# Gathers tied to chunk products by a one-column copy, and the prompt's odd projections spread over rounds

## The chip, the cores and the metric

The kernel runs on one core of one Trainium2 chip, as a single program of some 71,600 instructions. The metric is the device time of one execution in microseconds: the median over several executions. The five engines are named as the profile names them: PE is TensorE (PEld its weight loads), DVE is VectorE, ACT is ScalarE, POOL is GpSimd, SP is SyncE. Each works through its own instructions in order; between engines, semaphores hold an instruction back until what it reads is written.

## What is computed

The reference is one step of a trunk with two layers over two token groups: 128 prompt tokens (P) and 512 sample tokens (S), 1024 features each, in fp32. Every layer has a mixer and then an expert mixer ("PEER"). Layer 0's mixer is a Fourier and short convolution mixer; layer 1's ("odd") is a recurrence (RG-LRU) and a bidirectional RWKV-7 scan. The part that matters is the expert mixer: 16,384 experts, each one row of a table `u` and one of a table `v`; every token picks 8 x 16 of them.

```python
def _peer(h, wq, keys, u_tab, v_tab):
    ...
    idx = e1 * N_KEYS + e2                 # 8 x 16 experts per token
    gate = jax.nn.softmax(sc, axis=-1)
    def block(args):                       # 128 tokens at a time
        hb, ib, gb = args
        act = jax.nn.gelu(jnp.einsum('td,thkd->thk', hb, u_tab[ib]))
        return jnp.einsum('thk,thkd->td', gb * act, v_tab[ib])

def _rwkv_mix(z, mu, ...):                 # odd layer; z is a projection of the normed tokens
    zp = jnp.pad(z, ((0, 0), (1, 1), (0, 0)))
    z = z + mu * (0.5 * (zp[:, 0:S] + zp[:, 2:S + 2]) - z)
    r, k, v = z[..., 0:o1], z[..., o1:o2], z[..., o2:o3]
    wd, ad, gd = z[..., o3:o4], z[..., o4:o5], z[..., o5:]
```

## The kernel before

**Two ways through the experts.** Sample blocks 1 to 3 (384 tokens) go through all 16,384 experts densely. The prompt's block and sample block 0 (128 tokens each) gather: for each of 128 slots, one indirect DMA brings one row of `u` or `v` per token (128 x 1024 fp32, 0.52 MB) into a tile `g`, and VectorE reduces it: a dot product with the token's input for `u` (L1138), an accumulation into `h2P` or `h2S` for `v` (L1168, here called an accumulation). `gather` (the indirect DMA is L1152) issues it from GpSimd's queue.

**The stages in time.** The even mixers run to about 500 us, the routing of layer 0 to 1025, its dense stage to 1895, the odd mixers from there to about 2940, then the end of the mixer and the routing of layer 1 to 3645, its dense stage to 4524, and closing work behind it.

**The dense stage** (`dense_peer`) loops over 128 chunks of 128 experts. Chunk c has a *hidden product*, hidden(c) (`hidden`, 24 matmuls at L1079, operands split into a high and a low fp32r part: `uhS`, `lwS`), a GELU into `geS` (L1252), the multiplication of `geS` by the dense gates `gt` (L1276, called the product of the chunk below, on VectorE), a split of that into `ah` (ScalarE) and `al` (VectorE, L1279), and 18 value matmuls (L1285) against `vh` and `lwS`, the two parts of the chunk's rows of `v`. hidden(c) is made AHEAD = 4 chunks early. For half of the chunks it has been computed during routing already and *spilled* to DRAM as `ged`; in runs of four, so that four chunks compute it and the next four read it back. Both `uhS`/`vh` weight tiles (`w`, 0.5 MB each) come through SP's DMA queue with few buffers, and `split` makes the two parts: `vh` or `uhS` on ScalarE (L1222), `lwS` on VectorE (L1224).

**What decides when a gather is issued.** Gathers are tasks in a list, `B.tasks`; `B.left` counts the slots left. `B.pump(n)` writes out n of them at that place of the program, and `defer` writes the reduction of a gather two gathers later. Their own waits are for the index tile, a free `g` buffer (four, and three more in the dense stage) and the order of GpSimd's queue. A scheduler then orders each engine's instructions by priorities and its own simulation, so that an accumulation need not stand where it was written. `B.pace(n, src)` does the same behind a copy of one column of `src` on GpSimd, into a tile `pace`; `issue_after` makes the gathers stand on GpSimd behind that copy, without a semaphore of their own. It was used in the mixers only.

In the dense stage the count per chunk spreads what is left over the chunks up to LAST = 122; in layer 0, OVER = 88 tasks are kept for the odd stage. `first` is the prompt's or sample's own task that must end by chunk 127.

**The odd stage** (`odd_mixers`, `run`) is a round robin over generators: `S.odd_wkv` gives the sample's scan units, which advance in turn by one `yield` per round, and beside them the generator `prompt` waits until no gather task is left, then finishes the prompt's layer 0 (`P.peer_out`) and starts the prompt's own projections: `P.odd_lora` (three), and `wkv_inputs` (three times four; one `yield` per four), which the prompt's first unit calls. A projection is `project` (eight 128 x 128 matmuls at L438 over `wblk`), then `shift` on VectorE and ScalarE.

Of the kernel before, what the change touches and what calls it, by code (L numbers as in the profile page):

```python
# [22 lines left out]
DEPTH = 2  # L23
# [124 lines left out]
class Body:  # L148
# [71 lines left out]
                f(*a)  # L220

    def pace(self, n, src):
        if self.tasks:
            p = self.tl([128, 1], "pace", 2)
            self.pump(n, self.nc.gpsimd.tensor_copy(p, src[:, 0:1]))

# [94 lines left out]
class Trunk:  # L321
# [286 lines left out]
    def odd_lora(self, l):  # L608
        nc, T, B, hT = self.nc, self.T, self.B, self.hT
        lo = []  # L610
        for i in range(3):
            z = self.zt()
            self.project(l, "in", hT, 20 + i, z[:, 1:T + 1])
            if self.S:
                B.pace(5, z[:, 1:2])
            o = B.mx([128, T], f"lo{i}" + self.tag)
            self.shift(z, o, 12 + i)
            lo.append(o)
        nc.scalar.activation(lo[0], lo[0], AF.Tanh)
        nc.scalar.activation(lo[2], lo[2], AF.Tanh, scale=0.5)  # L620
        nc.vector.tensor_scalar(lo[2], lo[2], 0.5, 0.5, OP.mult, OP.add)
        self.lo = lo
# [96 lines left out]
    def wkv_inputs(self, l, groups, g):  # L719
# [4 lines left out]
        for i in range(3):  # L724
            z = self.zt() if self.S else self.zt("zP", 3)
            if self.S:
                self.project(l, "in", hT, 8 + 4 * i + g, z[:, 1:T + 1])
                self.B.pace(5, z[:, 1:2])
                self.shift(z, z[:, 1:T + 1], 4 * i + g)
                rkv.append([z[:, 1:257], z[:, 257:513]])  # L730
            else:
                z = z.rearrange("p (a b) -> p a b", a=4)
                for hp in range(4):
                    self.project(l, "in", hT, 8 + 4 * i + hp, z[:, hp, 1:T + 1])
                    self.shift(z[:, hp, :], z[:, hp, 1:T + 1], 4 * i + hp)
                rkv.append([z[:, 0:2, 1:T + 1], z[:, 2:4, 1:T + 1]])
            yield
        halves, own = [], lambda n: (n, 4) if self.S else (n + "P", 2)
# [516 lines left out]
    def dense_peer(self, l, G, ges, first, f):  # L1255
# [4 lines left out]
        for c in range(128):  # L1260
            if c == 127:
                self.B.finish_task(first)
            elif c < LAST:
                more = self.B.left - (OVER if l < DEPTH - 1 else 0)
                self.B.pump(max(0, -(-more // (LAST - c))))
            if 0 not in f and first not in self.B.tasks:
                f[0] = self.halves(self.acc)
                self.finish(l, (0,), f, ("pB", 2))
# [5 lines left out]
            ge = ges[c]  # L1274
            g4 = lambda x: x.rearrange("p (b t) -> p b t", t=32)
            nc.vector.tensor_tensor(g4(ge), g4(ge), gt[:, :, c % 4, :], op=OP.mult)  # L1276
            ah, al = self.dt([128, N], "ah", 2, F32R), self.dt([128, N], "al", 2, F32R)
            nc.scalar.activation(ah, ge, AF.Copy)  # L1278
            nc.vector.tensor_tensor(al, ge, ah.bitcast(F32), op=OP.subtract)  # L1279
            vh, vl = self.split(self.dt, "vh", self.I["v"][l * NEXP + c * 128:l * NEXP + (c + 1) * 128])  # L1280
            for n in range(nd):
# [93 lines left out]
LAST, OVER = 122, 88  # L1375
# [111 lines left out]
def odd_mixers(B, l, P, S):  # L1487
# [6 lines left out]
    def prompt(own, side):  # L1494
# [3 lines left out]
            yield  # L1498
        yield from P.peer_out(l - 1)
        B.odd_rate = 3  # L1500
        P.odd_lora(l)
        lru, wkv = [P.odd_lru(l, c) for c in range(4)], list(P.odd_wkv(l))
        n = int(bool(side) and inspect.getgeneratorstate(side[0]) != inspect.GEN_CREATED)
        side[n:n] = lru
        own.extend(wkv)
        yield
        while any(g in own or inspect.getgeneratorstate(g) != inspect.GEN_CLOSED for g in lru + wkv):
# [11 lines left out]

    B.odd, B.odd_rate = True, 6  # L1520
    B.odd_constants()
    S.odd_lora(l)
    lru = [S.odd_lru(l, c) for c in range(4)]
    run(S.odd_wkv(l), prompt, lru, [modulations()] + [S.end_early(l, lru)] * 1,
        lambda n, a: (2 >= 0 or n % 2) * abs(2) if B.tasks and a else 2)

# [14 lines left out]
```

## Time and profile before

| | |
|---|---|
| median of 3 executions | 4566.64 us (4565.18 to 4579.20) |
| the profiled execution, its own time | 4558.22 us |
| its span, first to last instruction | 4556.4 us |
| mean granted TensorE clock | 0.902 of full speed |
| instructions | 71,571 |
| busy: TensorE, VectorE | 3837.5 us (84%), 3467.4 us (76%) |
| busy: ScalarE, GpSimd | 1757.4 us (39%), 1387.9 us (30%) |
| DMA | 1198 MB, 263 GB/s over the span |

A time of the metric is some two microseconds longer than the span between the first and last instruction. Busy shares are means over stages that have different limits, so no share of the whole tells what a change in one stage is worth; the rows in the section ahead of the prediction are cut by stage. Matmuls of fp32 operands are recorded twice, so that a projection of eight matmuls has 16 records.

### The profile page before, as it was taken

Reading aid. Unit: us, or ns where it says so; the run is one execution under the profiler, and the core shown is the slowest. Engines: PE = TensorE matmul, PEld = TensorE weight load, DVE = VectorE, ACT = ScalarE, POOL = GpSimd, SP = SyncE. Lnnn points to the kernel's source line nnn. Section 1 sums busy time; section 2 is a strip of 40 time slices with the busy share of each in tenths; the row PEclk is TensorE's granted clock in tenths of the full one; section 3 lists DMA queues with packets and bytes.
Section 4 is the critical chain, followed back from the end, with each engine's and each line's share of the span. In section 5 each row is a group of like instructions: output and inputs, shape, how many; then the busy total and the mean of one; then the engine's idle time right before and its main releaser. Section 6 shows DMA issues by size and latency. Waiting matters only on the chain. (4 is left out here: it accounts for less than half of the span.)

```text
span 4556.4 us, 71571 instructions
## 1 busy us (share of the span) xinstructions
PE 3837.5 (84%) x26326; PEld 3142.3 (69%) x26326; DVE 3467.4 (76%) x7480; ACT 1757.4 (39%) x3391; POOL 1387.9 (30%) x1105
## 2 busy tenths in 40 slices
PE   7977968999888999778889877719779888988897
PEld 4653767997766788634665654508779877877786
DVE  3398999987889744668554786589999787888845
ACT  2211235763322333244575543203357623332332
POOL 0044322434556200044000232253125354466300
PEclk9997989999999999887888877759999999999999
DMA  9699856999999755368531566487569999999853
GB/s 342 227 350 356 264 196 236 349 357 355 360 360 362 280 175 172 128 237 286 177 101 58 182 222 205 169 289 248 171 225 341 346 367 342 346 365 369 310 170 120
DMA packets 455551, 1198.05 MB, mean 263 GB/s; under 512 B 52848, under 2 KB 195312, under 8 KB 452128
## 3 DMA queue, kind: packets, MB, share of 16 engines
q1 hardware_dynamic: 307744, 656.54, 41.4%
q0 software_dynamic: 147456, 536.94, 32.8%
q8 instruction: 207, 3.39, 0.3%
q14 instruction: 144, 1.18, 0.1%
HBM read 1093.34 MB, written 99.98 MB: 262 GB/s over the span
## 5 line engine op out<-in xcount | busy, mean ns | idle before, releaser
L1079 PE MATMUL ps<-hiS,lwS 128*128 128x384 f32 (+1 forms) x2304 | 817.5, 356 | 81.2 <-DVE lwS L1224 80.9
L1079 PE MATMUL ps<-loS,uhS 128*128 128x384 f32 (+1 forms) x2432 | 857.9, 353 | 1.1 <-DVE loS L432 1.1
L1079 PE MATMUL ps<-hiS,uhS 128*128 128x384 f32 (+1 forms) x2304 | 813.2, 353 | 51.3 <-ACT geS L1252 26.0
L1079 PEld LDWEIGHTS ps<-hiS,lwS 128*128 128x128 f32 x2304 | 447.2, 194 | 111.7 <-DVE lwS L1224 101.4
L1222 ACT ACTIVATE uhS<-w 128x1024 fp32r<-128x1024 f32 x304 | 320.8, 1055 | 527.3 <-PE ps L1079 358.6
L1285 PE MATMUL ps<-vh,ah 128*128 128x512 f32 x1536 | 429.4, 401 | 99.9 <-ACT vh L1222 78.8
L1152 POOL DMA_INDIRECT g<-v,idxP x256 | 351.7, 1374 | 515.8 <-DVE h2P L1168 311.9
L1152 POOL DMA_INDIRECT g<-u,idxS x256 | 349.0, 1363 | 512.9 <-DVE g L1138 391.9
L1079 PEld LDWEIGHTS ps<-hiS,uhS 128*128 128x128 f32 x2304 | 447.5, 194 | 82.3 <-ACT uhS L1222 34.1
L1285 PE MATMUL ps<-lwS,ah 128*128 128x512 f32 x1536 | 483.4, 396 | 10.9 <-DVE lwS L1224 10.8
L1079 PEld LDWEIGHTS ps<-loS,uhS 128*128 128x128 f32 x2432 | 471.5, 194 | 24.0 <-DVE loS L432 3.7
L1285 PE MATMUL ps<-vh,al 128*128 128x512 f32 x1536 | 477.3, 393 | 0.0
L1224 DVE TENSOR_TENSOR lwS<-w,uhS 128x1024 fp32r<-128x1024 f32 x304 | 369.7, 1217 | 122.9 <-ACT uhS L1222 82.0
L1152 POOL DMA_INDIRECT g<-v,idxS x256 | 367.8, 1437 | 237.6 <-DVE h2S L1168 178.6
L1224 DVE TENSOR_TENSOR lwS<-w,vh 128x1024 fp32r<-128x1024 f32 x256 | 312.9, 1223 | 153.7 <-issue 79.3
L1152 POOL DMA_INDIRECT g<-u,idxP x256 | 291.7, 1139 | 414.2 <-DVE g L1138 183.2
L1285 PEld LDWEIGHTS ps<-vh,ah 128*128 128x128 f32 x1536 | 289.1, 192 | 167.1 <-ACT vh L1222 92.5
L1278 ACT ACTIVATE ah<-geS 128x384 fp32r<-128x384 f32 x256 | 134.3, 525 | 671.4 <-PE ps L1285 598.9
L1138 DVE SCALAR_TENSOR_TENSOR g<-g,h2P 128x1024 f32<-128x1024 f32 x256 | 310.2, 1216 | 81.4 <-DMA g<-u,idxP 81.0
L1168 DVE SCALAR_TENSOR_TENSOR h2P<-g,wtP,h2P 128x1024 f32<-128x1024 f32 x254 | 324.6, 1278 | 50.7 <-DMA g<-v,idxP 49.2
L1285 PEld LDWEIGHTS ps<-lwS,ah 128*128 128x128 f32 x1536 | 291.2, 191 | 81.6 <-DVE lwS L1224 20.1
L1285 PEld LDWEIGHTS ps<-vh,al 128*128 128x128 f32 x1536 | 291.4, 190 | 62.8
(480 smaller groups left out, 6687.9 us busy)
## 6 DMA issues: line engine op xcount, KB each, us to landing
w<-ut SPq DMA_DIRECT2D x256, 512.0 KB
w<-v SPq DMA_DIRECT2D x256, 512.0 KB
w<-wblk SPq DMA_DIRECT2D x142, 512.0 KB
w<-wmod SPq DMA_DIRECT2D x96, 512.0 KB
gt<-G SPq DMA_DIRECT2D x64, 768.0 KB
w<-wout SPq DMA_DIRECT2D x56, 512.0 KB
ged<-geS SPq DMA_DIRECT2D x128, 192.0 KB
G<-fa SPq DMA_DIRECT2D x12, 2048.0 KB
```

The costliest lines, as they stand in the source:

```text
L1079: self.nc.tensor.matmul(out, a[:, s], b[:, k, :], start=k == 0 and i == 0, stop=k == 7 and i == 2)
L1138: self.nc.vector.scalar_tensor_tensor(u, u, 1.0, self.h2[t], OP.mult, OP.mult, accum_out=self.act[t][:, s:s + 1])
L1152: self.nc.gpsimd.indirect_dma_start(out=g, out_offset=None, in_=self.I[tab], in_offset=bass.IndirectOffsetOnAxis(ap=self.idx[t][:, s:s + 1 ...
L1168: nc.vector.scalar_tensor_tensor(acc, v, w[:, s:s + 1], acc, OP.mult, OP.add)
L1222: self.nc.scalar.activation(h, raw, AF.Copy)
L1224: self.nc.vector.tensor_tensor(lo, raw, h.bitcast(F32), op=OP.subtract)
L1278: nc.scalar.activation(ah, ge, AF.Copy)
L1285: nc.tensor.matmul(outs[n][h], a[:, s], b[:, 512 * h:512 * h + 512], start=c == 0 and i == 0, stop=c == 127 and i == 2)
```

## The change

It has two parts. In `dense_peer` the pump at the head of each chunk goes; behind `ah` there is now `B.pace(n, ge)` with the same count, so that each chunk's gathers stand on GpSimd behind a copy of one column of the gated `geS`, which waits for the chunk's product on VectorE. `pace` no longer makes a copy where no gather is due. In the odd stage the prompt's projections yield after each one (`odd_lora`, and three more yields per group in `wkv_inputs`), and `prompt` runs them itself, before the prompt's scan units are added to the list. The sample's own `odd_lora` is drained at once, as before.

```diff
@@ -220,7 +220,7 @@
                 f(*a)
 
     def pace(self, n, src):
-        if self.tasks:
+        if n and self.tasks:
             p = self.tl([128, 1], "pace", 2)
             self.pump(n, self.nc.gpsimd.tensor_copy(p, src[:, 0:1]))
 
@@ -616,6 +616,7 @@
             o = B.mx([128, T], f"lo{i}" + self.tag)
             self.shift(z, o, 12 + i)
             lo.append(o)
+            yield
         nc.scalar.activation(lo[0], lo[0], AF.Tanh)
         nc.scalar.activation(lo[2], lo[2], AF.Tanh, scale=0.5)
         nc.vector.tensor_scalar(lo[2], lo[2], 0.5, 0.5, OP.mult, OP.add)
@@ -733,6 +734,8 @@
                 for hp in range(4):
                     self.project(l, "in", hT, 8 + 4 * i + hp, z[:, hp, 1:T + 1])
                     self.shift(z[:, hp, :], z[:, hp, 1:T + 1], 4 * i + hp)
+                    if hp < 3:
+                        yield
                 rkv.append([z[:, 0:2, 1:T + 1], z[:, 2:4, 1:T + 1]])
             yield
         halves, own = [], lambda n: (n, 4) if self.S else (n + "P", 2)
@@ -1260,9 +1263,6 @@
         for c in range(128):
             if c == 127:
                 self.B.finish_task(first)
-            elif c < LAST:
-                more = self.B.left - (OVER if l < DEPTH - 1 else 0)
-                self.B.pump(max(0, -(-more // (LAST - c))))
             if 0 not in f and first not in self.B.tasks:
                 f[0] = self.halves(self.acc)
                 self.finish(l, (0,), f, ("pB", 2))
@@ -1276,6 +1276,9 @@
             nc.vector.tensor_tensor(g4(ge), g4(ge), gt[:, :, c % 4, :], op=OP.mult)
             ah, al = self.dt([128, N], "ah", 2, F32R), self.dt([128, N], "al", 2, F32R)
             nc.scalar.activation(ah, ge, AF.Copy)
+            if c < LAST:
+                more = self.B.left - (OVER if l < DEPTH - 1 else 0)
+                self.B.pace(max(0, -(-more // (LAST - c))), ge)
             nc.vector.tensor_tensor(al, ge, ah.bitcast(F32), op=OP.subtract)
             vh, vl = self.split(self.dt, "vh", self.I["v"][l * NEXP + c * 128:l * NEXP + (c + 1) * 128])
             for n in range(nd):
@@ -1498,10 +1501,11 @@
             yield
         yield from P.peer_out(l - 1)
         B.odd_rate = 3
-        P.odd_lora(l)
+        yield from P.odd_lora(l)
         lru, wkv = [P.odd_lru(l, c) for c in range(4)], list(P.odd_wkv(l))
         n = int(bool(side) and inspect.getgeneratorstate(side[0]) != inspect.GEN_CREATED)
         side[n:n] = lru
+        yield from P.wkv_inputs(l, P.inputs, 0)
         own.extend(wkv)
         yield
         while any(g in own or inspect.getgeneratorstate(g) != inspect.GEN_CLOSED for g in lru + wkv):
@@ -1519,7 +1523,8 @@
 
     B.odd, B.odd_rate = True, 6
     B.odd_constants()
-    S.odd_lora(l)
+    for _ in S.odd_lora(l):
+        pass
     lru = [S.odd_lru(l, c) for c in range(4)]
     run(S.odd_wkv(l), prompt, lru, [modulations()] + [S.end_early(l, lru)] * 1,
         lambda n, a: (2 >= 0 or n % 2) * abs(2) if B.tasks and a else 2)
```

On VectorE, in the dense stage of layer 0, around the product of chunk 104 (`geS_13917` before, `geS_14114` after; line numbers of the kernel after are larger by three here; `lwS<-w,uhS` is the low part of a chunk's `u` weights, `lwS<-w,vh` that of its `v` weights). Before:

```order
L1276 TENSOR_TENSOR geS_13917<-geS_13917,gt_14146 128x384
L1224 TENSOR_TENSOR lwS_14020<-w_14016,uhS_14018 128x1024
L1279 TENSOR_TENSOR al_14051<-geS_13816,ah_14050 128x384
L1224 TENSOR_TENSOR lwS_14058<-w_14054,vh_14056 128x1024
L1276 TENSOR_TENSOR geS_13982<-geS_13982,gt_14146 128x384
L1224 TENSOR_TENSOR lwS_14085<-w_14081,uhS_14083 128x1024
L1279 TENSOR_TENSOR al_14116<-geS_13850,ah_14115 128x384
L1224 TENSOR_TENSOR lwS_14123<-w_14119,vh_14121 128x1024
```

After:

```order
L1276 TENSOR_TENSOR geS_14114<-geS_14114,gt_14351 128x384
L1227 TENSOR_TENSOR lwS_14221<-w_14217,uhS_14219 128x1024
L1282 TENSOR_TENSOR al_14252<-geS_14009,ah_14251 128x384
L1171 SCALAR_TENSOR_TENSOR h2P_13102<-g_14361,wtP_13099,h2P_13102 128x1024
L1227 TENSOR_TENSOR lwS_14264<-w_14260,vh_14262 128x1024
L1276 TENSOR_TENSOR geS_14181<-geS_14181,gt_14351 128x384
L1227 TENSOR_TENSOR lwS_14288<-w_14284,uhS_14286 128x1024
L1282 TENSOR_TENSOR al_14319<-geS_14045,ah_14318 128x384
L1171 SCALAR_TENSOR_TENSOR h2P_13102<-g_14397,wtP_13099,h2P_13102 128x1024
```

Before, no accumulation stands in this part of the stage; after, each product has behind it `lwS`, `al` and the accumulation (`h2P`, L1171) of one gather, and then the low part of the next chunk's weights.

On GpSimd, the gathers of the prompt's values in the same stage (`g` is the tile that a gather fills). Before, at the end of the queue of this stage:

```order
L1152 DMA g_14348<-v,idxP_1447 128x1024
L1152 DMA g_14413<-v,idxP_1447 128x1024
L1152 DMA g_14478<-v,idxP_1447 128x1024
L1152 DMA g_14543<-v,idxP_1447 128x1024
L1152 DMA g_14579<-v,idxP_1447 128x1024
```

After:

```order
L225 COPY pace_14321<-geS_14045 128x1
L1155 DMA g_14323<-v,idxP_1447 128x1024
L225 COPY pace_14359<-geS_14114 128x1
L1155 DMA g_14361<-v,idxP_1447 128x1024
L225 COPY pace_14395<-geS_14181 128x1
L1155 DMA g_14397<-v,idxP_1447 128x1024
```

Gather `g_14361` stands behind the copy that reads `geS_14114`, and its accumulation is the one (`h2P_13102<-g_14361`) in the rows of VectorE above, behind that product and ahead of the next.

On TensorE, in the odd stage, where the prompt's projections (L438, `fa` the prompt's normed tokens, `w` a weight block) start beside the sample's scan units (L882 to L1018 before, L885 to L1014 after). Before, the last of 16 projections and what follows:

```order
L438 MATMUL ps_17896<-fa_17298,w_17894 128x128 x8
L438 MATMUL ps_17967<-fa_17298,w_17965 128x128 x8
L438 MATMUL ps_17985<-fa_17298,w_17983 128x128 x8
L438 MATMUL ps_18003<-fa_17298,w_18001 128x128 x8
L708 MATMUL ps_18084<-cst,zP_17964 128x128
L686 MATMUL ps_18091<-r_3654_17911,bd_17907 128x128
L686 MATMUL ps_18094<-r_3654_17911,bd_17907 128x128
L1008 MATMUL ps_18099<-wst_18097,l_3607_17644 64x64 x2
L920 MATMUL ps_18103<-l_3442_16779,l_3441_16778 32x32 x4
L438 MATMUL ps_18021<-fa_17298,w_18019 128x128 x8
L708 MATMUL ps_18084<-cst,zP_17964 128x128
L920 MATMUL ps_18103<-l_3442_16779,l_3441_16778 32x32 x4
```

After, the last of eight in one piece and what follows:

```order
L438 MATMUL ps_18033<-fa_17542,w_18031 128x128 x8
L438 MATMUL ps_18045<-fa_17542,w_18043 128x128 x8
L438 MATMUL ps_18068<-fa_17542,w_18066 128x128 x8
L687 MATMUL ps_18206<-r_3764_18060,bd_18056 128x128
L687 MATMUL ps_18209<-r_3764_18060,bd_18056 128x128
L1011 MATMUL ps_18233<-wst_18231,l_3733_17907 64x64 x2
L923 MATMUL ps_18237<-l_3564_17023,l_3563_17022 32x32 x5
L438 MATMUL ps_18141<-fa_17542,w_18139 128x128 x8
L923 MATMUL ps_18237<-l_3564_17023,l_3563_17022 32x32 x3
L895 MATMUL ps_18249<-e_3687_17666,ra_18015 64x64
L438 MATMUL ps_18215<-fa_17542,w_18213 128x128 x8
L895 MATMUL ps_18249<-e_3687_17666,ra_18015 64x64 x3
```

Eight projections stand in one piece where 16 stood, and of the others each has matmuls of the units on both sides.

## Rows read from the trace of the kernel before

**Rows 1.** The page: busy tenths of TensorE and DMA in 40 slices.

```profile
PE   7977968999888999778889877719779888988897
...
DMA  9699856999999755368531566487569999999853
```

**Rows 2.** Windows, dense stage of layer 0, blocks of eight chunks; columns first.

```profile
core 0: us, PE busy (x) PEld busy (x) DVE busy (x) ACT busy (x) POOL busy (x), PEclk, DMA share, GB/s
1024.80:1079.80 55.00, 46.10 (x200) 38.92 (x199) 36.52 (x56) 14.06 (x20) 19.48 (x16) 0.90 0.96 356
1079.80:1130.80 51.00, 50.48 (x246) 44.38 (x245) 42.75 (x64) 19.73 (x26) 24.62 (x18) 1.00 0.98 348
...
1312.20:1377.80 65.60, 54.10 (x241) 44.30 (x240) 56.29 (x58) 17.78 (x25) 39.24 (x28) 0.95 0.98 361
...
1441.60:1504.10 62.50, 51.84 (x237) 42.08 (x235) 62.32 (x93) 17.00 (x24) 36.62 (x27) 1.00 1.01 376
...
1713.10:1895.00 181.90, 181.90 (x873) 159.44 (x872) 85.07 (x104) 65.74 (x89) 0.00 (x0) 1.00 0.52 166
sum 870.20, PE 797.34 PEld 681.38 DVE 611.87 ACT 279.06 POOL 281.32; mean PE 61.33 PEld 52.41 DVE 47.07 ACT 21.47 POOL 21.64
```

**Rows 3.** Windows, dense stage of layer 1, same columns.

```profile
3763.10:3829.60 66.50, 53.46 (x240) 44.95 (x239) 51.20 (x79) 17.41 (x25) 33.97 (x26) 0.92 0.94 340
...
3980.70:4031.40 50.70, 49.91 (x240) 43.14 (x238) 44.29 (x56) 17.28 (x25) 28.34 (x21) 1.00 1.00 367
...
4159.10:4223.80 64.70, 55.03 (x240) 47.62 (x240) 56.33 (x57) 18.04 (x25) 41.76 (x29) 0.92 0.99 362
...
4392.20:4441.80 49.60, 49.60 (x242) 43.80 (x241) 23.04 (x29) 18.09 (x25) 0.00 (x0) 1.00 0.55 175
...
sum 879.40, PE 805.69 PEld 696.97 DVE 665.05 ACT 277.75 POOL 355.02; mean PE 53.71 PEld 46.46 DVE 44.34 ACT 18.52 POOL 23.67
```

**Rows 4.** Waits of TensorE, 1026 to 1540 us: total us, times, longest.

```profile
PE ps L1285 <- ACT vh L1222: 48.2, 23, 6.6
```

**Rows 5.** DMA, 3192 to 3306 us: volume; gathers, median us to landing.

```profile
DMA packets 7372, 19.59 MB, mean 172 GB/s; under 512 B 816, under 2 KB 2864, under 8 KB 7363
...
g<-v,idxP POOLq DMA_INDIRECT x11, 4.6
```

**Rows 6.** DMA of 684 to 798 us, the same two lines.

```profile
DMA packets 7576, 26.98 MB, mean 237 GB/s; under 512 B 847, under 2 KB 2639, under 8 KB 7183
...
g<-u,idxS POOLq DMA_INDIRECT x20, 7.2
```

**Rows 7.** DMA of 1938 to 2052 us, the same two lines.

```profile
DMA packets 7598, 26.51 MB, mean 233 GB/s; under 512 B 1109, under 2 KB 1109, under 8 KB 7593
...
g<-v,idxP POOLq DMA_INDIRECT x41, 5.7
```

**Rows 8.** Timeline of GpSimd (start, us, idle before); then `pace`, ns min/median/max.

```profile
2754.59 0.18 POOL L225 COPY pace<-e 128x1 f32<-128x1 f32 x1 [10.10 <-DVE e L860]
2755.28 1.02 POOL L1152 DMA_INDIRECT g<-u,idxP  x1 [0.50 <-issue]
...
L225 POOL COPY pace<-e x12: 181/619/1102, 2037.1 to 2853.4; 128x1 f32<-128x1 f32 x12
```

**Rows 9.** Lines: busy us, mean ns of one, idle time before.

```profile
L1224 DVE TENSOR_TENSOR lwS<-w,uhS 128x1024 fp32r<-128x1024 f32 x304 | 369.7, 1217 | 122.9 <-ACT uhS L1222 82.0 <-PE ps L1285 38.4 <-PE ps L424 2.2
...
L1168 DVE SCALAR_TENSOR_TENSOR h2P<-g,wtP,h2P 128x1024 f32<-128x1024 f32 x254 | 324.6, 1278 | 50.7 <-DMA g<-v,idxP 49.2
...
L1279 DVE TENSOR_TENSOR al<-geS,ah 128x384 fp32r<-128x384 f32 x256 | 142.0, 555 | 123.7 <-ACT ah L1278 120.6 <-PE ps L1285 3.1
```

**Rows 10.** Timeline of TensorE: four projections (64 records).

```profile
2208.05 10.02 PE L438 MATMUL ps<-fa,w 128*128 128x128 f32 x64 [0.16 <-DVE z L627]
```

**Rows 11.** Windows in odd stage and routing of layer 1, columns as above.

```profile
2200.00:2262.00 62.00, 52.41 (x488) 47.13 (x488) 22.93 (x102) 30.22 (x78) 0.00 (x0) 0.89 0.61 186
...
3080.00:3420.00 340.00, 290.27 (x1515) 260.97 (x1516) 334.23 (x1148) 145.33 (x295) 73.61 (x57) 0.94 0.64 215
```


## The prediction, made before the change was timed

> **What bounds the kernel now.** The page came first: TensorE is busy for 84% of the span, and its row of tenths falls below 9 in stretches where the DMA row is at 9 [rows 1]. The two dense stages (1025 to 1895 us and 3645 to 4524 us) take 870.2 and 879.4 us of the 4556.4. I then cut each into blocks of eight chunks, at the start of every eighth `al` (the split of the activations). The gather pattern of the schedule repeats in eights, because four chunks compute their hidden product and the next four read it back. A block without any gather's accumulation takes 49.6 us with TensorE busy throughout and the DMA queues at 0.55 [rows 3]: this is the floor. A block with 16 to 19 accumulations costs hardly more, 50.7 to 51.0 us [rows 2, 3]. One with 28 takes 64.7 to 65.6 us; there DMA is at 0.98 to 0.99, VectorE is busy for 56.3 us, and TensorE idles for 10 us or more [rows 2, 3]. In the first part of that stage TensorE waits most for `vh`, the split of the value weights [rows 4]; so the weights come late because gathers share the queues. Per block, counted in the instruction order of before (accumulations between one eighth `al` and the next): layer 0 has 16, 17, 19, 28, 28, 28, 28, 26, 17 and then none; layer 1 has 17, 28, 25, 16, 17, 17, 19, 28, 28, 28, 28, 4 and none. The gathers run as early as buffers allow, and the last third of each stage has none. Excess over the floor is about 77 us in layer 0 and 86 us in layer 1 (sums less 16 floors, the last block being seven chunks at 33 us). That is what a more even spread can win.
>
> **Dense stages: what the new order does.** Counted in the same way, the order of after has 16, 17, 19, 28, 28, 24, 12, 8, 8, 8, 6, 9, 8, 8, 8, 0 in layer 0, and 20, 15, 22, 23, 23, 19, 17, 22, 28, 28, 15, 14, 8, 8, 8, 0 in layer 1. The front is unchanged: gathers pumped during routing are still queued there, and no copy holds them. Behind it there is about one per chunk. Layer 1 has 15 more in all, which come out of the odd and routing stages.
>
> Priced by blocks alone, this is a gain: 24 lies between 19 and 26, by the line between 50.7 and 62.5 us at 59 us; blocks of 6 to 16 would be at the floor.
>
> **The wait that is added.** In the paced part each gather stands on GpSimd behind a copy that waits for its chunk's product `geS`, and VectorE's order holds that gather's accumulation in front of the next group of products (the rows of VectorE in the section on the change). VectorE is in order, so product, copy, gather, landing, accumulation and next product form a loop. Per eight chunks the products come in five groups (104; 105; 106; 107 to 109; 110 and 111), each with the accumulations of its own gathers behind it: five round trips. What waits behind the accumulation on VectorE is `lwS` and `al` of the chunks that TensorE does next.
>
> One round trip: product's end to copy between nothing and the 0.50 us that stands between copy and gather, of which I take 0.15; copy 0.18, gap 0.50 [rows 8], 0.85 us together; then issue to landing. That was 4.6 us where the queues moved 172 GB/s, 5.7 at 233, 7.2 at 237 [rows 5 to 7]. A paced block moves the 175 GB/s of the floor [rows 3] and eight gathers of 0.52 MB in some 53 us, 79 GB/s: 254. I take 5.7, the median of a stretch of steady gathers; the 7.2 is from a stretch of bursts. Both ends stay for the range.
>
> VectorE's own work on the loop, by 1.28 for an accumulation, 1.22 for `lwS`, 0.55 for a product and for `al` [rows 9]: after each of the first two groups accumulation, `lwS`, product, 3.05; after the third accumulation and product, 1.83; after the fourth the second gather's later issue (1.5), accumulation, `al`, `lwS`, accumulation, product, 6.4; after the fifth 1.5, accumulation, `al`, two `lwS`, product, 6.3. Together 20.7. A block is 5 x (0.85 + 5.7) + 20.7 = 53.5 us, against the floor's 49.6. At 4.6 us it is 48.0, so the floor rules; at 7.2 it is 61.0.
>
> Layer 0: the first five blocks as before, 1024.8 to 1312.2, 287.4 us [rows 2]; 59; nine paced at 53.5, 481.5; the last 33.1 (181.9 less three floors [rows 2, 3]) and 1 for a late accumulation. Sum 862, that is -8 us. Layer 1: 52 and 50 for 20 and 15; four of 22 or 23 halfway between 50.7 and 62.5, 226; 19 and 17, 101; two of 28, 129; five paced, 267; 34. Sum 860, that is -19. Dense stages together -27; each microsecond of landing time moves it by 14 x 5 = 70 us. The copies themselves (244, 0.18 us) lie on GpSimd, which idles; without that cover they would only lengthen the round trip, which the 0.85 already holds. The last tile's closing work, put at chunk 88 in layer 1 before, comes some 30 chunks later, still ahead of the last chunk's end in the order, under TensorE's 33 us; so the tail of the kernel stays.
>
> The DMA page of the Trainium skill (DMA: Bandwidth & Descriptors, section Anatomy of one DMA) fits a gather-path transfer by 2.0 us plus its bytes over 436 GB/s: 3.2 us for 0.52 MB, an estimate by that page. By it a block is 5 x 4.05 + 20.7 = 41 us, so the floor rules and the sum is that of the first rival. No stretch of this trace shows a median so low; the rows decide for 4.6 or more.
>
> **Odd stage.** Before, 16 of the prompt's projections stand in one piece on TensorE; the first four take 10.0 us [rows 10]. In 2200 to 2262 us TensorE is busy 52.4 of 62 us and VectorE only 22.9: the sample's units stand still behind them [rows 11]. After, eight are still in one piece, and the other nine have unit work between. The work is the same; what can be won is TensorE's idle 9.6 us in that window and a little overlap: -8, bounds -30 to +15, the loss if a late weight load blocks the units' matmuls behind it. The prompt comes later, and 21 of its accumulations (1.28 us each, 27 us of VectorE) leave the odd stage: worth some -9. Six of them go to routing, where VectorE is busy 334 of 340 us [rows 11]: +7. The other 15 are counted in layer 1. The odd stage gives -10. The lines for an empty pump and for the sample's projections change no order that I could find ahead of the first dense stage.
>
> **Sum.** -27 - 10 = -37 us against the profiled execution's 4558.2 us (span 4556.4 and 1.8 around it): 4521. The median of the runs, 4566.6, is 1.0018 times it, so 4529 us. No change means here within 0.3%, 14 us.
>
> **Rivals.**
> Free round trips: landing at 4.6 us or less, since the gathers come singly. Every paced block is at the floor, 14 x 3.9 = 55 us better: -92, 4474 us by the median. For it: the queues are at 0.55 without gathers. Against: that 4.6 was at 172 GB/s [rows 5], and a paced block asks the queues for 254. Chance 0.20.
>
> The loop takes the place of the DMA limit (slower): at 7.2 us each paced block is 61.0, 14 x 7.5 = 105 us worse: +68, 4634 us. It decides from 6.4 us on, where the total is +14. For it: 7.2 at 237 GB/s [rows 6], and copies in the trace that took up to 1.1 us, median 0.62 behind VectorE's `e` [rows 8], which adds to each of the five trips: 0.6 us more would do the same as 0.6 us of landing. Beside this stands the page SBUF — State Buffer of the Trainium skill (section Who interferes with whom): a VectorE operation with two inputs in SBUF holds off GpSimd's reads, and whoever issues first blocks the other for its whole length. The next `lwS` is such an operation; if every copy waited for one, that page would have each trip 1.2 us longer. The copies of the trace agree in part: many are at 0.18. Chance 0.23.
>
> Nothing measurable: landing of 6.0 to 6.4 us, or blocks of 22 and 23 that already cost 64 us, as one of 25 did (66.5), which takes 30 of the 37. 4553 to 4580 us. Chance 0.15.
>
> **How the numbers follow.** My forecast has 0.42, and with the first rival faster has 0.62; same 0.15; slower 0.23. Likeliest 4529, its own range 4495 to 4552. The range for 8 in 10 goes from short of the free case's full sum to two thirds of the slow one: 4460 to 4605.
>
> **What would show it.** Right: blocks in the last third of each dense stage at 52 to 55 us with VectorE waiting for gathers (`h2P` or `h2S` waiting for the DMA of `g`), the same blocks of 28 in front, DMA near 0.75 behind; 2200 to 2300 us with VectorE busier. Wrong: paced blocks at 49.6 (no loop), or at 60 and more; or front blocks that grew, because copies delay gathers there too; or a TensorE that still idles ten microseconds around the prompt's projections.

## The result, and the profile after

The changed kernel takes 4639.25 us (median of 4, 4631.22 to 4644.07); the kernel before, in the same comparison, 4572.11 (4565.18 to 4579.20). The ratio is 1.0145, interval 1.012 to 1.017: slower by about 67 us or 1.5%, clear of the noise, where I had forecast 4529 and given 0.23 to the case that it comes out slower, at 4634. The profiled execution has a span of 4635.1 us against 4556.4, which is +78.7, and falls apart at the first and last `al` of each dense stage as follows: +5.2 ahead of the first dense stage (where the order is unchanged; with routing as it was, that start lies between 1022.9 and 1034.2 us in the profiles of this study), +56.7 in it, -15.3 in the odd and routing stages, +31.9 in the second dense stage, nothing behind it.

The dense stage of layer 0, the window view with the columns of [rows 2], the first block, and of the later ones those that have 12, 8, 9 and 8 accumulations:

```profile
1030.10:1086.90 56.80, 47.68 (x200) 39.84 (x199) 36.48 (x57) 13.92 (x20) 28.36 (x30) 0.89 0.96 359
...
1371.10:1423.20 52.10, 52.03 (x255) 45.86 (x254) 36.12 (x42) 18.54 (x25) 21.80 (x18) 1.00 0.83 288
...
1485.40:1547.10 61.70, 55.20 (x241) 47.31 (x240) 31.46 (x37) 17.83 (x24) 16.13 (x16) 0.89 0.60 209
...
1677.30:1742.20 64.90, 54.84 (x248) 46.98 (x247) 32.90 (x39) 18.13 (x24) 15.52 (x16) 0.92 0.60 199
...
1804.10:1866.10 62.00, 54.15 (x241) 46.19 (x241) 31.52 (x37) 17.87 (x24) 17.08 (x16) 0.92 0.60 208
...
sum 926.50, PE 824.49 PEld 702.42 DVE 602.95 ACT 279.47 POOL 361.97; mean PE 51.53 PEld 43.90 DVE 37.68 ACT 17.47 POOL 22.62
```

Before, the full blocks behind the last accumulation cost 49.5 to 50.6 us each (49.6 in [rows 3]). Now a block with seven to nine of them takes 61.7 to 66.7 us, as much as one of 28 did. DMA is at 0.6, VectorE is busy for half the time, and TensorE idles 8 us in the block from 1804 us (its own work takes 54.2 us there in place of 49.6, where the granted clock has a mean of 0.92 in place of 1.00). No engine and no queue is full, which points to a chain of waits; the experiments test it. The dense stage of layer 1, blocks of 20, 23, 28 and 8:

```profile
3691.40:3751.90 60.50, 48.77 (x202) 40.85 (x201) 41.63 (x54) 14.38 (x20) 31.81 (x32) 0.89 0.98 369
...
3865.80:3925.00 59.20, 53.96 (x242) 46.75 (x243) 49.76 (x75) 18.92 (x26) 35.09 (x31) 0.94 0.99 358
...
4217.70:4283.20 65.50, 55.20 (x240) 46.30 (x240) 56.86 (x57) 17.60 (x25) 36.85 (x32) 0.95 0.91 330
...
4507.40:4573.00 65.60, 54.21 (x248) 46.44 (x247) 35.17 (x44) 17.99 (x24) 17.00 (x16) 0.94 0.58 202
...
sum 911.40, PE 819.26 PEld 701.68 DVE 680.29 ACT 277.01 POOL 440.66; mean PE 51.20 PEld 43.86 DVE 42.52 ACT 17.31 POOL 27.54
```

VectorE's accumulations, the view by line with its idle time before them, after and then, for `h2S`, before:

```profile
L1171 DVE SCALAR_TENSOR_TENSOR h2S<-g,wtS,h2S 128x1024 f32<-128x1024 f32 x254 | 325.7, 1282 | 205.9 <-DMA g<-v,idxS 203.6
L1171 DVE SCALAR_TENSOR_TENSOR h2P<-g,wtP,h2P 128x1024 f32<-128x1024 f32 x254 | 325.0, 1280 | 171.0 <-DMA g<-v,idxP 170.2
...
L1168 DVE SCALAR_TENSOR_TENSOR h2S<-g,wtS,h2S 128x1024 f32<-128x1024 f32 x254 | 325.5, 1281 | 3.2
```

VectorE now waits 374 us in all for values to land; before it was 49 for `h2P` [rows 9] and at most 3.2 for `h2S`. One block of the first dense stage, GpSimd's timeline (start, duration, and in brackets the idle time before and its releaser), the first copy and the first gather of each trip:

```profile
1804.36 0.38 POOL L225 COPY pace<-geS 128x1 f32<-128x1 f32 x1 [7.26 <-DVE geS L1276]
1805.04 1.63 POOL L1155 DMA_INDIRECT g<-v,idxP  x1 [0.30 <-issue]
1813.74 0.38 POOL L225 COPY pace<-geS 128x1 f32<-128x1 f32 x1 [7.07 <-DVE geS L1276]
1814.42 0.96 POOL L1155 DMA_INDIRECT g<-v,idxP  x1 [0.30 <-DVE geS L1276]
...
1828.54 3.13 POOL L225 COPY pace<-geS 128x1 f32<-128x1 f32 x1 [9.90 <-DVE geS L1276]
1831.82 0.97 POOL L1155 DMA_INDIRECT g<-v,idxP  x1 [0.16 <-DVE lwS L1227]
...
1845.53 1.51 POOL L225 COPY pace<-geS 128x1 f32<-128x1 f32 x1 [10.47 <-DVE geS L1276]
1847.20 0.97 POOL L1155 DMA_INDIRECT g<-v,idxP  x1 [0.16 <-issue]
1856.31 1.04 POOL L225 COPY pace<-geS 128x1 f32<-128x1 f32 x1 [8.15 <-DVE geS L1276]
1857.51 1.10 POOL L1155 DMA_INDIRECT g<-v,idxP  x1 [0.16 <-issue]
1866.34 0.38 POOL L225 COPY pace<-geS 128x1 f32<-128x1 f32 x1 [7.73 <-DVE geS L1276]
```

and VectorE's in the same block, the products (`geS`, with their number behind the shapes) and the accumulation that ends the wait of each trip:

```profile
1803.68 0.55 DVE L1276 TENSOR_TENSOR geS<-geS,gt 128x384 f32<-128x384 f32 x1
...
1811.85 1.28 DVE L1171 SCALAR_TENSOR_TENSOR h2P<-g,wtP,h2P 128x1024 f32<-128x1024 f32 x1 [6.01 <-DMA g<-v,idxP]
1813.05 1.49 DVE L1276 TENSOR_TENSOR geS<-geS,gt 128x384 f32<-128x384 f32 x3
...
1821.13 1.28 DVE L1171 SCALAR_TENSOR_TENSOR h2P<-g,wtP,h2P 128x1024 f32<-128x1024 f32 x1 [4.99 <-DMA g<-v,idxP]
...
1827.86 1.02 DVE L1276 TENSOR_TENSOR geS<-geS,gt 128x384 f32<-128x384 f32 x2
...
1838.37 1.29 DVE L1171 SCALAR_TENSOR_TENSOR h2P<-g,wtP,h2P 128x1024 f32<-128x1024 f32 x1 [4.15 <-DMA g<-v,idxP]
...
1844.84 0.55 DVE L1276 TENSOR_TENSOR geS<-geS,gt 128x384 f32<-128x384 f32 x1
...
1853.29 1.29 DVE L1171 SCALAR_TENSOR_TENSOR h2P<-g,wtP,h2P 128x1024 f32<-128x1024 f32 x1 [6.29 <-DMA g<-v,idxP]
...
1855.62 0.55 DVE L1276 TENSOR_TENSOR geS<-geS,gt 128x384 f32<-128x384 f32 x1
...
1863.32 1.28 DVE L1171 SCALAR_TENSOR_TENSOR h2P<-g,wtP,h2P 128x1024 f32<-128x1024 f32 x1 [5.54 <-DMA g<-v,idxP]
...
1865.66 0.55 DVE L1276 TENSOR_TENSOR geS<-geS,gt 128x384 f32<-128x384 f32 x1
```

The products come in five groups, and from one group to the next pass 9.4, 14.8, 17.0, 10.8 and 10.0 us: together the 62.0 us of the block. Each group waits behind an accumulation whose gather was issued behind the copy of the group ahead. That is the loop of the prediction, trip by trip.

### The profile page after: what moved, and what is told of

The parts are those of the page before. It is cut to its first block, busy times and chain, and to the rows that moved or that the text cites. A ratio compares the mean times of both kernels' runs of the same rounds, so it can differ in the third digit from the quotient of the medians.

```text
span 4635.1 us, 72047 instructions
## 1 busy us (share of the span) xinstructions
PE 3882.0 (84%) x26326; PEld 3164.4 (68%) x26326; DVE 3457.2 (75%) x7480; ACT 1756.2 (38%) x3389; POOL 1546.1 (33%) x1326
## 5 line engine op out<-in xcount | busy, mean ns | idle before, releaser
L1288 PE MATMUL ps<-lwS,ah 128*128 128x512 f32 x1536 | 504.2, 411 | 89.6 <-DVE lwS L1227 89.5
L1288 PE MATMUL ps<-vh,al 128*128 128x512 f32 x1536 | 494.0, 404 | 0.0
L1171 DVE SCALAR_TENSOR_TENSOR h2S<-g,wtS,h2S 128x1024 f32<-128x1024 f32 x254 | 325.7, 1282 | 205.9 <-DMA g<-v,idxS 203.6
L1171 DVE SCALAR_TENSOR_TENSOR h2P<-g,wtP,h2P 128x1024 f32<-128x1024 f32 x254 | 325.0, 1280 | 171.0 <-DMA g<-v,idxP 170.2
L1288 PEld LDWEIGHTS ps<-lwS,ah 128*128 128x128 f32 x1536 | 300.8, 199 | 170.6 <-DVE lwS L1227 107.0
L1155 POOL DMA_INDIRECT g<-v,idxS x256 | 346.8, 1355 | 124.8 <-DVE h2S L1171 63.9
L225 POOL COPY pace<-geS 128x1 f32<-128x1 f32 x244 | 172.8, 711 | 637.0 <-DVE geS L1276 612.9
```

Source lines behind the costliest of these rows:

```text
L1155: self.nc.gpsimd.indirect_dma_start(out=g, out_offset=None, in_=self.I[tab], in_offset=bass.IndirectOffsetOnAxis(ap=self.idx[t][:, s:s + 1 ...
L1171: nc.vector.scalar_tensor_tensor(acc, v, w[:, s:s + 1], acc, OP.mult, OP.add)
L1288: nc.tensor.matmul(outs[n][h], a[:, s], b[:, 512 * h:512 * h + 512], start=c == 0 and i == 0, stop=c == 127 and i == 2)
```

## Experiments

**The change in its two parts.** The dense stage's copies with the odd stage of before, and the odd stage's order with the dense stages of before, as differences from the changed kernel:

```diff
-        yield from P.odd_lora(l)
+        P.odd_lora(l)
...
-        yield from P.wkv_inputs(l, P.inputs, 0)
```

```diff
+            elif c < LAST:
+                more = self.B.left - (OVER if l < DEPTH - 1 else 0)
+                self.B.pump(max(0, -(-more // (LAST - c))))
...
-                self.B.pace(max(0, -(-more // (LAST - c))), ge)
```

> The dense stages of the changed kernel (gathers behind a copy of the chunk's product) with the odd stage of before. From the profiles the change costs +57 us in the first dense stage, +32 in the second, gives 15 in the stages between, and +5 stand ahead of the first dense stage. If the parts are independent, this kernel is some 15 us slower than the changed one: about 4650 us, with dense stages of 920 to 930 and 905 to 915 us. If the odd stage's new order has nothing to do with the 15 us (they come from gathers that moved out of it), this kernel takes 4640 or less.

> The prompt's odd projections one per round, with the dense stages of before. If the new order of the projections is worth TensorE's idle time of 9.6 us around them, 4555 to 4565 us against 4572 of before. If it is worth nothing, within 5 us of before. Dense stages as before, 870 and 880 us, in both cases.

The dense part alone: 4661.15 us, ratio 1.018 (1.0153 to 1.0208). The odd part alone: 4558.27 us, 0.9966 (0.9947 to 0.9985). The odd part is within its range; the dense part is 11 us above its forecast, with a second dense stage of 923.6 us where I expected 905 to 915. The parts add up (+84 and -19 against +67 for the two together): the loss is all in the dense stages, and the odd part is worth some 15 to 22 us. But the idle time that I had looked at, around the projections, stays. The odd part's kernel in the window of [rows 11], and then the stretch from the last `al` of layer 0 to the last output projection (L502), before and with the odd part:

```profile
2200.00:2262.00 62.00, 51.73 (x584) 45.67 (x584) 30.62 (x127) 30.57 (x77) 0.00 (x0) 0.87 0.52 159
...
1894.60:2975.40 1080.80, 861.03 (x11443) 584.73 (x11442) 730.26 (x2069) 490.07 (x1053) 231.42 (x260) 0.78 0.54 180
...
1890.90:2964.80 1073.90, 859.79 (x11443) 577.11 (x11442) 710.09 (x2027) 489.47 (x1052) 207.93 (x216) 0.79 0.51 171
```

TensorE idles 10.3 us in the window, no less than before; what is new is that 584 records instead of 488 pass in it, and VectorE works 30.6 us instead of 22.9. The scan units move while the projections run. Over the whole stretch TensorE's idle time falls from 219.8 to 214.1 us, so most of the 6.9 us won there is idle time after all, only not in that window.

**The accumulations later.** Only the place of the accumulations on VectorE is changed, by an order without a wait:

```diff
-            if c < LAST:
-                more = self.B.left - (OVER if l < DEPTH - 1 else 0)
-                self.B.pace(max(0, -(-more // (LAST - c))), ge)
-            nc.vector.tensor_tensor(al, ge, ah.bitcast(F32), op=OP.subtract)
+            split = nc.vector.tensor_tensor(al, ge, ah.bitcast(F32), op=OP.subtract)
+            if c < LAST:
+                more = self.B.left - (OVER if l < DEPTH - 1 else 0)
+                with self.B.tc.issue_after(split.ins):
+                    self.B.pace(max(0, -(-more // (LAST - c))), ge)
```

What a chunk's pump writes out on VectorE is the accumulation of the gather two chunks earlier; `issue_after` puts it behind this chunk's `al`, so that four to six products stand on VectorE between a paced gather's own product and its accumulation in most cases of this run's first dense stage, where the changed kernel has none to two.

> The changed kernel with one difference: in the dense stage the accumulations written out at a chunk stand on VectorE behind that chunk's split of the activations (al), and each belongs to a gather of two chunks earlier. The copies, the gathers and their counts stay. Loop theory (product, copy, gather, landing, accumulation, next product): the landing no longer stands between products, so paced blocks of eight chunks fall from 62 to 67 us to 50 to 52, blocks of 16 to 23 accumulations in the second dense stage from 56 to 60 to 51 to 55, and the kernel to 4450 to 4490 us. Rival, the queues or the copies themselves are the limit: nothing in that changes here, paced blocks stay at 60 or more and the kernel at 4620 to 4650.

4482.88 us, ratio 0.9806 (0.9777 to 0.9835): the loop theory's range, and 1.9% faster than the kernel before. A paced block, and the DMA view of the paced stretch (volume, then the gathers' median from issue to landing):

```profile
1784.60:1834.20 49.60, 49.60 (x242) 43.80 (x241) 32.04 (x37) 18.22 (x25) 12.68 (x14) 1.00 0.76 260
```

```profile
DMA packets 52378, 102.64 MB, mean 253 GB/s; under 512 B 3314, under 2 KB 31986, under 8 KB 52353
...
g<-v,idxP POOLq DMA_INDIRECT x40, 5.7
...
g<-v,idxS POOLq DMA_INDIRECT x23, 5.8
```

Eight accumulations in 49.6 us with TensorE busy throughout: the floor. The same holds for ten of the eleven blocks with eight accumulations (49.6 to 50.0 us); the other, with the norm of sample block 0 in it, takes 65.6. The copies and the gathers are as many as in the changed kernel; only no product waits for a landing any more. This tells the theories apart: it is the chain. The expectation for the second stage's front was a miss: its eight blocks took 50.1 to 58.4 us, most of them above the 51 to 55 expected.

**Two copies.** The chain's price, from the copy's side:

```diff
-            self.pump(n, self.nc.gpsimd.tensor_copy(p, src[:, 0:1]))
+            self.nc.gpsimd.tensor_copy(p, src[:, 0:1])
+            q = self.tl([128, 1], "pace", 2)
+            self.pump(n, self.nc.gpsimd.tensor_copy(q, src[:, 0:1]))
```

> The changed kernel with a second copy of the same column behind the first, ahead of the gathers. A copy has a mean of 0.71 us in the changed kernel's trace and 0.16 to 0.30 us of gap behind it. Loop theory: each round trip is longer by 0.35 (a free copy) to 1.0 us; five trips in each of some 14 paced blocks and as many in the blocks of the second stage's front make +25 to +100 us, so 4665 to 4740. Rival, the blocks are limited by the queues or by TensorE's waits for weights and not by a chain that the copy is in: within 10 us of 4639, since GpSimd idles two thirds of the time.

4649.48 us (4638.96 to 4658.46), ratio 1.0158 (1.0131 to 1.0184): 10 us above the changed kernel (some 6 by the two ratios, whose intervals overlap), at the edge of the rival's range and below mine. The five blocks of layer 0 that are undisturbed by closing work rise from 61.9 to 64.4 us on average, 0.5 us for each trip, which is the low end expected; but the second dense stage came out 8 us shorter, ahead of its paced blocks, and the total says little. As a test of the chain it is weak.

**No copy, the same wait.** VectorE writes one column into the gather's tile, and the gather waits for that:

```diff
...
         else:
             g = B.tl([128, D], "g", GW)
+        if B.touch is not None:
+            self.nc.vector.tensor_copy(g[:, 0:1], B.touch[:, 0:1])
...
-                self.B.pace(max(0, -(-more // (LAST - c))), ge)
+                self.B.touch = ge
+                self.B.pump(max(0, -(-more // (LAST - c))))
+                self.B.touch = None
```

> The changed kernel, accumulations where they were, but the wait is made without an instruction on GpSimd: VectorE writes one column of the product into the gather's own tile behind the product, and the gather waits for that. In a paced block of the changed kernel's trace (1804 to 1866 us) the copies that end a round trip take 0.38, 0.38, 3.13, 1.51 and 1.04 us, 6.4 together, against 0.9 in my sum. If these long copies (which lie beside VectorE's two-input operations) are in the loop, paced blocks fall from 62 to 56 to 58 us and the kernel to 4570 to 4610. If only the landing counts and a copy's length is hidden, they stay at 61 or more, and the kernel at 4625 or more. The scheduler also places gathers of the front otherwise here, so the paced blocks are the test, the total is second.

4656.14 us, ratio 1.0176 (1.016 to 1.0192): the second branch by the time, but not its reason, as the rows below show. The front was placed otherwise (the first block of the two dense stages took 92.4 and 154.2 us), so the total says little. The last seven blocks of eight in layer 0 took 58.4 to 65.7 us, 61.9 on average against 63.2 in the changed kernel. The changed kernel's gathers in its paced stretch, from the DMA view, and then those of this kernel, with three of its issues on GpSimd's timeline:

```profile
DMA packets 52714, 103.90 MB, mean 208 GB/s; under 512 B 3343, under 2 KB 32015, under 8 KB 52687
...
g<-v,idxP POOLq DMA_INDIRECT x40, 6.5
...
g<-v,idxS POOLq DMA_INDIRECT x24, 6.7
```

```profile
DMA packets 52257, 102.22 MB, mean 211 GB/s; under 512 B 3297, under 2 KB 31969, under 8 KB 52231
...
g<-v,idxP POOLq DMA_INDIRECT x40, 7.8
...
g<-v,idxS POOLq DMA_INDIRECT x24, 7.9
```

```profile
1762.34 1.01 POOL L1159 DMA_INDIRECT g<-v,idxP  x1 [10.08 <-DVE g L1158]
1763.66 3.63 POOL L1159 DMA_INDIRECT g<-v,idxP  x1 [0.30 <-issue]
1779.40 1.70 POOL L1159 DMA_INDIRECT g<-v,idxP  x1 [12.11 <-DVE g L1158]
```

Without the copies, the landing counted from the issue is 1.2 to 1.3 us longer, at the same load. Counted over the trips of the eight paced blocks of layer 0 whose accumulation waits over 2 us (36 and 34), the issue comes 0.9 us earlier (1.17 us behind the product's start against 2.10), and the accumulation 0.7 us later behind the issue (7.12 against 6.44). Of that 0.7 the issue's own length has 0.2 (1.38 against 1.20; single ones took 3.63 and 1.70 where about 1.0 is usual), and the rest lies behind it. So a trip is only 0.25 us shorter without its copy; why the transfer then lands later is not shown.

**The copies without the loop, and the spread.** The kernel with later accumulations was run without copies (`pump` in place of `pace`), and with fewer gathers queued ahead of the dense stages:

```diff
-                B.rate = 2
+                B.rate = 1        # and 0 in another kernel
```

> The kernel with the later accumulations, without any copy in the dense stage: the gathers are written out at the same place of the program and wait only for a free tile. If the place of the accumulations on VectorE is what spreads the gathers (a tile comes free with its accumulation), the copies add nothing: within 15 us of 4483. If the copies do the spreading, gathers run ahead again and the gain over the kernel before goes: 4540 to 4580.

> The kernel with the later accumulations, and one gather in place of two written out at each weight split of the routing stages, so that fewer are left queued at the front of the dense stages: by the instruction order 15 or 16 accumulations in nearly every block of the first dense stage and 16 to 24 in the second. Blocks of 16 have cost 50.2 to 51.0 us and blocks of 24 about 58. So the first dense stage 820 to 840 us, the second 845 to 860, and 53 accumulations (1.28 us each) fewer ahead of the first and 29 fewer between them, which gives up to 105 us where VectorE is the limit there. 4390 to 4480 us. Rival, routing waits for TensorE or the queues and not for VectorE: only the dense stages gain, 4470 to 4490.

> As the kernel with one gather for each split, with none: 19 to 30 accumulations in nearly every block of both dense stages, 137 fewer ahead of the first dense stage and 112 fewer between the two than in the kernel with two. Blocks of 24 at 58 us make the dense stages 900 to 930 us each, +80 to +90 against the later accumulations with two. VectorE's 249 x 1.28 = 319 us leave the other stages; if VectorE is the limit there throughout, 4320 us, if half the time, 4480. I expect 4400 to 4480, and more than with one gather.

Without copies 4488.10 us, ratio 0.9817 (0.9798 to 0.9836): the same as with them. A tile comes free with its accumulation, and by this run the accumulations' place is enough to spread the gathers. One gather per split: 4497.21 us, 0.9832 (0.9811 to 0.9853), no gain: the first dense stage fell to 820.2 us as expected, but the second took 884.6, its blocks of 24 accumulations 60 to 71 us. None: 4581.49 us, 1.0027 (1.0013 to 1.004); 77 us were won ahead of the first dense stage and 46 between the two, but the dense stages took 941.3 and 957.4. Both were misses: I had not expected blocks of 24 to cost more than 58 us.

**Even counts.** Rounding up put 24 into each of the first blocks of layer 1; here each chunk's count follows a straight line, with one gather per split in both layers, and with one in layer 0 and two in layer 1:

```diff
+                total = more if c == 0 else total
                 with self.B.tc.issue_after(split.ins):
-                    self.B.pace(max(0, -(-more // (LAST - c))), ge)
+                    self.B.pace(max(0, more - total * (LAST - 1 - c) // LAST), ge)
...
-                B.rate = 2
+                B.rate = 1        # 1 + l in the other kernel
```

> The kernel with later accumulations and one gather per weight split in routing, and the counts per chunk laid out evenly (before, each was rounded up, so that 24 accumulations stood in each of the first blocks of the second dense stage and 16 in the rest): 17 in a block of the first dense stage, 19 or 20 in a block of the second. Blocks of 16 to 19 cost 49.5 to 51 us, so if the count per block is what sets its time, the first dense stage stays at 815 to 825 us, the second falls from 884 to 815 to 845, and the kernel from 4497 to 4430 to 4460 us. If something else made the blocks of 24 in the second stage slow (60 to 71 us there, against about 58 in the kernel before), such as the dot products of the first gathers, they stay slow with 20, and the kernel at 4475 or more.

> The same, with two gathers per weight split in the routing of layer 1: 14 to 23 accumulations in a block of the second dense stage, five of its blocks at 21 to 23. By count the second dense stage takes 835 to 850 us; routing of layer 1 has 32 accumulations more, which cost nothing if VectorE has room there (53 fewer ahead of the first dense stage gave 6 us). 4440 to 4475 us. If the slow blocks came from something else, 4465 to 4490.

With one in both: 4483.50 us, 0.9819 (0.9798 to 0.9841), the branch in which the count does not settle a block's time. The second dense stage took 886.3 us; its blocks, each of 19 or 20:

```profile
4191.70:4249.50 57.80, 51.90 (x241) 45.27 (x241) 44.94 (x47) 17.71 (x25) 30.43 (x27) 0.94 0.90 323
4249.50:4307.60 58.10, 52.78 (x242) 44.73 (x241) 45.93 (x48) 18.16 (x26) 33.25 (x28) 0.97 0.94 341
4307.60:4359.90 52.30, 50.48 (x242) 43.57 (x241) 45.90 (x49) 17.91 (x25) 33.86 (x28) 1.00 0.90 326
```

The last two differ by 6 us at one count of 20, with DMA at 0.90 to 0.94, and another block of 20 in this stage took 49.6 us; a block of 19 had cost 50.7 us before [rows 3]. Which order or collision makes them slow stays open. Mixed: 4466.03 us, 0.9776 (0.9754 to 0.9797), within its range, but also within that of its rival; the dense stages took 820.5 and 844.1 us, the second as the count had it. It is the fastest kernel of this study, 2.2% below the kernel before; against the later accumulations alone (0.9806) the intervals overlap.

## Why the prediction was wrong

The mechanism was there, and its price was too low. Against the sum of the prediction, from the same cuts:

| part | forecast, us | measured, us |
|---|---|---|
| layer 0, first five blocks | 287.4 | 285.0 |
| sixth (24 accumulations) | 59 | 56.0 |
| nine paced blocks | 481.5 | 556.8 |
| last | 34.1 | 28.7 |
| layer 1, eight blocks of 15 to 23 | 429 | 460.8 |
| two of 28 | 129 | 130.8 |
| five of 15, 14, 8, 8, 8 | 267 | 289.8 |
| last | 34 | 29.8 |
| odd and routing stages | -10 | -15.3 |

**What held.** The order's five round trips per block, what stands behind each on VectorE, the 0.15 us from a product's end to its copy (0.13), the unchanged front of layer 0, the sign of the odd stage's gain, and that the odd part and the dense part have nothing to do with one another.

**The step that failed** is the sentence "copy 0.18, gap 0.50, 0.85 us together; then issue to landing", with the choice "I take 5.7". In the block from 1804 us, the copies that begin the five trips take 0.38, 0.38, 3.13, 1.51 and 1.04 us, 6.4 together where I had 0.9: +5.5. From the issue to the accumulation pass 6.8, 6.7, 6.6, 6.1 and 5.8 us, 32.0 where I had 28.5: +3.5. The rest of the loop is 62.0 - 6.4 - 32.0 = 23.6 us, forecast as 20.7 + 5 x 0.67 = 24.0. So 53.5 + 5.5 + 3.5 - 0.5 = 62.0 us, which is the block. Some eight such blocks in layer 0 and three in layer 1 make about 98 of the 116 us by which the two dense stages exceed the forecast, if the blocks of 12, 14 and 15 are counted with them. It is the rival "the loop takes the place of the DMA limit", which I had put at 61.0 us a block and 4634 us.

**Why the trip is longer** can be read beside the copy of 3.13 us (1828.54 to 1831.67). VectorE in those microseconds, behind the two products that start at 1827.86:

```profile
1828.80 0.55 DVE L1282 TENSOR_TENSOR al<-geS,ah 128x384 fp32r<-128x384 f32 x1
1829.27 1.22 DVE L1227 TENSOR_TENSOR lwS<-w,vh 128x1024 fp32r<-128x1024 f32 x1
1830.40 1.22 DVE L1227 TENSOR_TENSOR lwS<-w,uhS 128x1024 fp32r<-128x1024 f32 x1
1831.99 0.56 DVE L1282 TENSOR_TENSOR al<-geS,ah 128x384 fp32r<-128x384 f32 x1 [0.37 <-ACT ah L1278]
```

The copy is released by the first of the two products; VectorE then goes on without a pause through the second, `al` and two `lwS`, each with two inputs, to about 1831.6; the copy ends at 1831.67, and VectorE's next instruction starts at 1831.99. The copies of 1.51 and 1.04 us lie likewise beside `lwS`, and end 0.05 us behind an instruction of VectorE. I had taken 0.18, the shortest copy of [rows 8], although the same group showed a median of 0.62 and up to 1.1 us in a like place, and kept the longer ones for the rival. The Trainium skill (SBUF — State Buffer, section Who interferes with whom) says that a VectorE operation with two SBUF inputs holds off a GpSimd instruction that reads SBUF; the rows above agree with it, with 3.13 us. So does a count over the 244 copies of the changed kernel's dense stages: the 54 with no VectorE instruction beside them took 0.17 to 0.20 us; the 180 that began while a two-input operation ran have a median of 0.81 and a maximum of 4.73, and 173 of these end within 0.06 us of the end of a VectorE instruction. In this loop most copies begin so, since the accumulation has just let VectorE's work go. No run took those operations away, so this is a sorting of one trace and not an experiment; and the kernel without copies shows that a trip wins only 0.25 us by losing its copy. Why the landing took 6.5 to 6.7 us at a mean load of 208 GB/s stays open: the issue's length explains part of it (1.63 us in the first trip, where 0.96 is usual). The 5.7 us itself was not a bad figure: where the loop is cut, at 253 GB/s, the gathers land in 5.7 us again. The Trainium skill's fit for such a transfer (DMA: Bandwidth & Descriptors, section Anatomy of one DMA), 3.2 us as an estimate, stands against 6.5 to 6.7 us here.

**The front of layer 1** was priced by counts, in which the dot products of `u` rows stand as accumulations, and its blocks of 15 to 20 took 52.6 to 60.5 us; it makes 32 us of the miss. This is a second step that failed, the price of a block by its count, and its waits are not those of the loop: in these eight blocks (3691.4 to 4152.3 us) VectorE waits for no value's landing, and for `u` rows only this (total us, times, longest):

```profile
DVE g L1141 <- DMA g<-u,idxS: 5.6, 6, 2.0
```

With the accumulations later the eight blocks took 440.8 us in place of 460.8, so their order has a part in it that no row here explains; blocks of 22 to 24 still took 54 to 58 us, about the line that I had drawn, and those of 16 and 18 took 55.9. DMA is at 0.95 on average in these eight blocks. What sets the time of such a block is open, as it is for the even counts.

**The odd and routing stages** gave 15 us by the profiles, where the forecast was 10; that is near partly by luck. To the last output projection (L502) it is 13 us (1080.8 to 1067.6) for 17 forecast, and behind it 2 us of gain, where six accumulations moved to routing were to cost 7. With the odd part alone the stretch to L502 falls by 7 us, and the idle time of the window in the step stayed at 10 us.

Two sentences of the prediction need a correction that changes no other number. Its excess over the floor (77 and 86 us) takes off 16 full floors; with the last block at 33 us, as it says, it is 93 and 102. And the range's lower end, 4460 us, lies beyond the free case's 4474 and not short of it.

## What to carry to other kernels

When a transfer is queued behind a marker of some compute, look where the consumer of that transfer stands on the engine that makes the marker: if it stands in front of the next marker, each transfer's whole latency is in series with the work, however idle all queues are. Order the consumer a few steps behind, which here needed no wait and no marker at all. A price for a round trip is taken from instances in the same neighbourhood, not from the shortest ones, since a loop brings the same neighbours together every time.

## What the runs showed of the hardware

A one-column copy on GpSimd took 0.17 to 0.20 us with VectorE idle beside it, and a median of 0.81 us when it began beside a two-input VectorE operation; one took 3.13 us beside four such operations in a row. The issue of an indirect gather behaves likewise in the changed kernel: 0.93 to 0.97 us for the 114 with no VectorE instruction beside them, a median of 1.63 for the 672 that began beside a two-input one. With the copy taken away, single issues took 1.70 and 3.63 us, and landings counted from the issue had medians of 7.8 and 7.9 us against 6.5 and 6.7, at the same 208 to 211 GB/s.
